# Two of the four float32 head tiles cast on chip before their TensorE transpose, and a planner that queues two engines on one PSUM bank

## Chip and metric

The kernel runs on one core of a Trainium2 chip. The metric is device time in microseconds (us); lower is better. Engines are named as in the profile: PE is TensorE (PEld its weight loads), DVE is VectorE, ACT is ScalarE, POOL is GpSimd, SP is the SyncE queue that issues most DMAs.

## What is computed

```python
batch, m, k, n = 16, 512, 1024, 768        # x, w1, w2: float32, drawn from randn
y1 = np.matmul(x, w1)
y2 = np.matmul(x, w2)
return (np.tanh(y1) * y2).astype(np.float32)
```

x flattened is 8192 x 1024; both products are 8192 x 768.

## The kernel before

**Tiles.** The 8192 rows are 64 row tiles of 128 (`mt`). A row tile must be transposed to `xT` (k on the partitions, 8 blocks of 128 columns) before TensorE can use it as the stationary operand. All products are in float16 and sum in float32 in eight PSUM banks of 128 x 512.

**Three stages.** Tiles 0 to 5 are the head and tile 63 the tail: their products are plain (`m{mt}{t}{F|G|M}{k}`: t is the weight matrix, F its first 512 columns, G its last 256, M both G parts side by side, k one of 8 slices). Tiles 6 to 62 go in 19 triples. A triple is 3 x 2 blocks of x (a row tile, half of k), the weights are 2 x 3 blocks of 512 columns (half of k; F of w1, F of w2, both G), and a scheme of 15 products of sums does the work of the plain 18: `A_SUMS` are sums of x blocks (`S{v}.{i}`, float16, DVE), `B_SUMS` sums of weight blocks (`B{v}`, once, DVE), and `C_OPS` is the list of what follows for each triple i: products `p*` (four matmuls each), `copy*` and `seed*` on ACT (a bank to SBUF, or a bank to another bank on which TensorE then accumulates), `add*` on DVE, and for each tile tanh (`t`, `th`, ACT) and multiplication (`m`, `mh`, DVE). In `C_OPS` names `c0` to `c10` are banks of a triple and `s...` SBUF tiles. Two entries matter here because they read the same bank: `t0` (ACT) and `add60` (DVE) both read `c0` after `p0`; in the same way `th1` (ACT) and `add4` (DVE) both read `c1` after `p3`. `p4` needs `add60`.

**The four ways of x onto the chip.** Tiles 0 to 3 are loaded as float32 (`Lx{mt}`, L332, by SP) and transposed by TensorE in float32 in two halves (`PT{mt}0`, `PT{mt}1`, L349: four transposes each into a bank of its own); each half is evacuated with a cast to float16 (`e{mt}0`, `e{mt}1`, L340 on ACT or L342 on DVE). Tiles 4 and 5 are loaded by POOL with a cast to float16 in the DMA (`L{mt}`, L382), transposed by TensorE in float16, eight transposes into one bank (`PT{mt}`, L359), and evacuated in one copy (`T{mt}`). Tiles 6 to 63 are loaded in the same way and transposed by DMA (L385, on SP). The POOL loads start behind a gate, which waits for weight slice b2 (L519). For each tile ACT sums the absolute values (`D{mt}`, L388), and for each weight slice too (`aw*`); these sums are needed only for a flag at the end, which chooses a general path for inputs out of range.

**Loads of the head.** In the order `x0 a0 x1 a1 x2 a2 x3 a3 a4 ... a7 b0 ... b7`, a0 to a3 from the ACT queue, the rest from SP, where a is w1 and b is w2 by k slices of 128 x 768 float32. Each slice is cast to float16 (`ca{k}`, `cb{k}`, L342 on DVE or L340 on ACT).

**The planner.** The order of the instructions on every engine is worked out in Python before the program is written, and pinned. `Planner.run` keeps a time for each engine; it offers every ready operation to each engine that may run it, with a duration for each engine, and takes the one that can start first. Between offers of equal start the engine listed first wins (`none, pe, act, dve, pool, sp`), and on one engine, among operations that start within 0.02, the one due first; ACT and DVE also hold back an operation for a more urgent one that becomes ready soon. The products of the triples keep one fixed order on TensorE (`PE_ORDER`); plain products of the tail tile may be put between the last of them (`FILL`) and are taken where the next fixed product can't start yet. A "chain" is the life of one PSUM bank: an operation that begins one takes the bank that was free first, and the bank comes free when the last operation of the chain has ended. Before the change the planner lets any two operations of one chain overlap that don't need each other. The durations it uses here:

```python
op(f"c{a}{k}", {"dve": 0.5, "act": 0.74}, ...)        # weight casts
op(f"e{mt}{h}", {"dve": 0.6, "act": 0.5}, ...)        # evacuation of half a float32 tile
op(f"T{mt}", {"dve": 0.67, "act": 0.93}, ...)         # evacuation of a float16 tile
```

What the planner does not write are the waits in the program: the tile framework adds those.

**Memory.** `xfpool` holds the float32 tiles in four rotating buffers; it is closed, with the pool of float32 weights, when the `pools` operation comes up in the plan, and the space is used for output tiles and `s...` tiles of the triples.

Of the kernel before, what the change touches and what calls it, by code (L numbers as in the profile page):

```python
# [77 lines left out]
class Planner:  # L78
# [13 lines left out]
    def op(self, name, engines, due, needs, fn, *args, behind=(), issued=(), chains=(), xfer=0.0, latency=None, seeds=False):  # L92


        assert name not in self.ops, name
        self.ops[name] = dict(engines=engines, due=due, needs=[n for n in needs if n], behind=[n for n in behind if n], issued=[n for n in issued if n], fn=fn, args=args,
                              chains=chains, xfer=xfer, latency=latency, seeds=seeds)
        for c in chains:
            self.chains.setdefault(c, {"left": 0, "bank": None, "end": 0.0})["left"] += 1

    def backward(self, margin):
        users = {n: [] for n in self.ops}
# [32 lines left out]
    def run(self, soon):  # L135
        free = {"none": 0.0, "pe": 0.0, "act": 0.0, "dve": 0.0, "pool": 0.0, "sp": 0.0}
        port = {"dve": 0.0, "pool": 0.0}
        bandwidth = 1.6
        left = {n: len(o["needs"] + o["behind"] + o["issued"]) for n, o in self.ops.items()}
        ready_at, end, engine_of, start_of = dict.fromkeys(self.ops, 0.0), {}, {}, {}  # L140
        ready = {e: [] for e in free}

        def release(n):
            for e in self.ops[n]["engines"]:
                ready[e].append(n)

        for n in self.ops:
            if not left[n]:
                release(n)
        position, lag = 0, 0.0  # L150
        strict = set(self.strict)
        while len(end) < len(self.ops):
            best = None
            for e, names in ready.items():
                options = []
                for n in names:
                    if n in strict and n != self.strict[position]:
                        continue
                    o = self.ops[n]
                    s = max(free[e], ready_at[n])  # L160
                    if n[0] in soon:
                        s = max(s, o["due"] + lag - soon[n[0]])
                    if e in port and n[0] in "SB":
                        s = max(s, port["dve" if e == "pool" else "pool"])
                    new = [c for c in o["chains"] if self.chains[c]["bank"] is None]
                    if new:
                        fit = self.fitting(o)
                        if not fit:
                            continue
                        s = max(s, min(fit)[0])  # L170
                    options.append((s, o["due"], n))
                if not options:
                    continue
                first = min(options)[0]
                s, due, n = min((o for o in options if o[0] <= first + 0.02), key=lambda o: o[1])
                ahead = max(0.4, self.LOOK * self.ops[n]["engines"][e])
                urgent = [o for o in options if o[0] < first + ahead and o[1] + lag < min(due + lag, o[0] + 1.0)]
                if urgent and e != "pe":
                    s, due, n = min(urgent, key=lambda o: o[1])
                if best is None or s < best[0]:  # L180
                    best = s, e, n
            if not best:
                held = [c for c, v in self.chains.items() if v["bank"] is not None and v["left"]]
                print("held", [(c, self.chains[c]["left"], [n for n, o in self.ops.items() if c in o["chains"] and n not in end][:4]) for c in held], free)
            assert best, ("stuck", [(n, self.ops[n]["needs"]) for n in self.strict[position:position + 3]])
            s, e, n = best
            o = self.ops[n]
            for c in o["chains"]:
                if self.chains[c]["bank"] is None:
                    entry = min(self.fitting(o))  # L190
                    self.bank_free.remove(entry)
                    self.chains[c]["bank"] = entry[1]
                    if not o["seeds"]:
                        (self.partial.add if c[0] == "T" else self.partial.discard)(entry[1])
            f = s + o["engines"][e]
            free[e] = f
            if e in port and n[0] in "SB":
                port[e] = f
            if o["xfer"]:
                bandwidth = max(bandwidth, f) + o["xfer"]  # L200
                done = bandwidth + (o["latency"] or self.LATENCY["cast" if e == "pool" else "sp"])
            else:
                done = f
            end[n], engine_of[n], start_of[n] = done, e, s
            for k in o["engines"]:
                ready[k].remove(n)
            if n in strict:
                position += 1
                lag = s - o["due"]
            for c in o["chains"]:  # L210
                chain = self.chains[c]
                chain["end"] = max(chain["end"], done + self.LATENCY[e])
                chain["left"] -= 1
                if not chain["left"]:
                    self.bank_free.append((chain["end"], chain["bank"]))
            for u in self.next.get(n, ()):
                ready_at[u] = max(ready_at[u], f)
                left[u] -= 1
                if not left[u]:
                    release(u)  # L220
            for u in self.users[n]:
                same = e in ("act", "dve", "pe") and e in self.ops[u]["engines"]
                slack = 1.0 if n in self.ops[u]["behind"] and self.ops[u]["xfer"] else 0.0
                ready_at[u] = max(ready_at[u], done + slack + (0.05 if same else 0.0 if o["xfer"] else self.LATENCY[e]))
                left[u] -= 1
                if not left[u]:
                    release(u)
        self.end, self.engine_of, self.start_of = end, engine_of, start_of
        return sorted(self.ops, key=lambda n: start_of[n])
# [3 lines left out]
def kernel(  # L233
# [18 lines left out]
    P = 128  # L252
    B, M, K = x.shape
    _, N = w1.shape
    KO = K // P
    KH = KO // 2
    MT = B * M // P
# [7 lines left out]
    WARM = 21  # L265
    SOON = {"S": 3.0, "D": 3.0}
    GATE = 2
    XH_FEW, XH_MORE = 3, ()
    POOL_FROM = 99
    BY_PE = 6  # L270
# [29 lines left out]

    head_stack = ExitStack()
    wfpool = head_stack.enter_context(tc.tile_pool(name="wf", bufs=WF_BUFS))
    xfpool = head_stack.enter_context(tc.tile_pool(name="xf", bufs=4))
    steady = {}

    pin = tc.keep_in_program_order
# [2 lines left out]
    op = plan.op  # L309
# [10 lines left out]
    def home(pool, key, shape, dtype):  # L320

        if (pool.name, key) not in fixed:
            fixed[pool.name, key] = pool.tile(shape, dtype, name=key)
        return fixed[pool.name, key]
# [3 lines left out]
        return xts[mt]  # L328

    def load_xf(e, mt):  # L330
        xfs[mt] = xfpool.tile([P, K], f32, tag="xf", name="x_f")
        pin(nc.sync.dma_start(xfs[mt], xf[mt]))  # L332

    def load_w(e, t, k, queue):
# [3 lines left out]
    def copy(e, dst, src):  # L338
        if e == "act":
            pin(nc.scalar.copy(dst, src))  # L340
        else:
            pin(engine[e].tensor_copy(dst, src))  # L342

    def cast_w(e, t, k):
        copy(e, wh[:, k, t * N:(t + 1) * N], wfs[t, k])

    def transpose_pe(e, mt, h, chain):
        for k in range(KH):
# [200 lines left out]
    for a, t, k in slices:  # L549
        op(f"c{a}{k}", {"dve": 0.5, "act": 0.74}, 6 + 1.3 * k + 9.5 * t,  # L550
           [f"L{a}{k}"], cast_w, t, k)
        op(f"aw{a}{k}", {"act": 0.92}, 80 + 10 * (t * KO + k), [f"c{a}{k}"], abs_w, t, k)
    for mt in range(4):
        for h in range(2):
            due = 5 + 2.3 * mt + 0.1 * h
            op(f"PT{mt}{h}", {"pe": 0.45}, due, [f"Lx{mt}"], transpose_pe, mt, h, ("T", mt, h), chains=[("T", mt, h)])
            op(f"e{mt}{h}", {"dve": 0.6, "act": 0.5}, due + 0.5, [f"PT{mt}{h}"] + ([f"e{mt}0"] if h else []), evacuate, mt, h,
               ("T", mt, h), chains=[("T", mt, h)])
        op(f"D{mt}", {"act": 1.05}, 30 + mt, [f"PT{mt}1"], abs_x, mt)

    PRODUCERS = {mt: [f"e{mt}0", f"e{mt}1"] if mt < 4 else [f"T{mt}"] for mt in range(MT)}
    xt_readers = {mt: [] for mt in range(MT)}

    def plain(mt, t, which, chain, due, at=0, first=True, behind=()):
        for k in range(KO):
            needs = ([f"cb{k}"] if t or which == "M" else []) + ([f"ca{k}"] if not t or which == "M" else [])
            needs.append(f"e{mt}{k // KH}" if mt < 4 else f"T{mt}")
            if not first and k == 0:
                needs.append(f"m{mt - 1}{t}{which}0")
            before = list(behind) + ([f"m{mt}{t}{which}0"] if k else [])  # L570
# [67 lines left out]
    for v, a, b, how in B_SUMS:  # L638
        needs = []
# [205 lines left out]
```

## Time and profile before

| what | value |
|---|---|
| time, median of 5 runs | 300.93 us (300.89 to 305.66) |
| time of the profiled execution | 303.9 us |
| span of its trace | 302.1 us |
| granted TensorE clock | 1.00 |
| PE busy | 293.2 us, 97% |
| DVE busy | 240.6 us, 80% |
| ACT busy | 220.2 us, 73% |
| POOL busy | 32.9 us, 11% |
| data moved | 64.80 MB, 214 GB/s mean |

The profile is of one execution. A row of its timeline has the start in us from the begin of the span, a duration, the engine, the line of the kernel, the operation, what it writes and reads by the program's names, shapes, and a count of merged instructions; in brackets, where the engine was idle before, how long and what ended that. Matmuls are pipelined: the duration of a row includes the last one's passage, so the stream's own pace is read from starts. A row of the windows view has a stretch of time, its length, the busy time and count of PE, PEld, DVE, ACT and POOL, the granted clock, the DMA share, and GB/s. In the page's slices each digit is the busy share of 1/40 of the span in tenths.

### The profile page before, as it was taken

To read this page: it belongs to the slowest core of one execution; us is meant where nothing else is said; L and a number is where in the kernel's file an instruction comes from. 1 tells how busy PE (TensorE), PEld (TensorE's weight loads), DVE (VectorE), ACT (ScalarE), POOL (GpSimd) and SP (SyncE) were. 2 spreads that over 40 slices of the span, in tenths; PEclk is the share of its full clock that TensorE was granted. 3 is DMA by queue.
4 is the path that set the end of the run, shared out by engine and by line. 5 is a ranking of instruction groups with operands and counts; after the bars stand their busy time and mean duration, and the time that the engine had idled before them with its cause. 6 is when DMAs were issued, how large, how long until landed. Compare 5 with 4: busy or idle time off the path is not lost. (4 is left out here: it accounts for less than half of the span.)

```text
span 302.1 us, 4458 instructions
## 1 busy us (share of the span) xinstructions
PE 293.2 (97%) x1418; PEld 138.9 (46%) x1418; DVE 240.6 (80%) x497; ACT 220.2 (73%) x438; POOL 32.9 (11%) x67
## 2 busy tenths in 40 slices
PE   8999999999999999799999999999999999999994
PEld 5656544444444444344444444444444444444442
DVE  1208999978988785988979779797898989888754
ACT  3879989998885965586777776778776777773641
POOL 0031220110101110201201101111010201000000
PEclk9999999999999999999999999999999999999999
DMA  7999999989999999999999999999999999995143
GB/s 291 407 400 189 167 162 183 178 164 206 193 209 161 232 259 82 127 298 221 273 233 207 197 199 177 293 213 191 234 205 227 204 207 225 211 378 204 69 176 125
DMA packets 82585, 64.80 MB, mean 214 GB/s; under 512 B 63616, under 2 KB 64128, under 8 KB 82560
## 3 DMA queue, kind: packets, MB, share of 16 engines
q1 hardware_dynamic: 73344, 47.20, 64.3%
q0 software_dynamic: 8640, 15.73, 35.6%
q10 hardware_dynamic: 576, 1.57, 1.3%
q8 instruction: 11, 0.18, 0.2%
q14 instruction: 14, 0.11, 0.2%
HBM read 39.85 MB, written 25.17 MB: 215 GB/s over the span
## 5 line engine op out<-in xcount | busy, mean ns | idle before, releaser
L475 PE MATMUL bank<-b,s 128*128 128x512 f16 x608 | 141.2, 379 | 2.4 <-DVE bank L490 2.3
L475 PEld LDWEIGHTS <-s 128*128 128x128 f16 x760 | 74.3, 98 | 92.8 <-issue 3.5
L490 DVE TENSOR_TENSOR bank<-bank,s 128x512 f32<-128x512 f32 x95 | 66.0, 695 | 26.4 <-ACT s L481 18.3
L481 ACT ACTIVATE s<-bank 128x512 f32<-128x512 f32 x95 | 55.2, 597 | 38.9 <-PE bank L475 38.9
L388 ACT ACTIVATE junk<-xh 128x1024 f16<-128x1024 f16 x60 | 63.4, 1056 | 3.0 <-DMA xh<-in_x_dram 2.8
L498 DVE TENSOR_TENSOR o<-o,bank 128x256 f32<-128x256 f32 (+1 forms) x114 | 61.1, 548 | 3.0 <-ACT o L493 2.4
L475 PEld LDWEIGHTS <-xT 128*128 128x128 f16 x380 | 37.1, 98 | 45.1 <-issue 0.8
L475 PE MATMUL bank<-b,xT 128*128 128x512 f16 x228 | 55.4, 379 | 0.0
L382 POOL DMA_DIRECT2D xh<-in_x_dram x60 | 32.1, 536 | 206.8 <-ACT o L493 63.1
L493 ACT ACTIVATE o<-bank 128x256 f32<-128x256 f32 x76 | 32.6, 437 | 11.9 <-DVE bank L490 8.6
L447 PE MATMUL bank<-wh,xT 128*128 128x512 f16 (+1 forms) x208 | 38.8, 338 | 1.4 <-ACT xT L340 0.7
L475 PE MATMUL bank<-wh,xT 128*128 128x512 f16 x152 | 39.0, 379 | 0.1
L475 PE MATMUL bank<-wh,s 128*128 128x512 f16 x152 | 39.0, 379 | 0.0
L432 DVE TENSOR_TENSOR s<-s,xT 128x512 f16<-128x512 f16 x76 | 31.7, 417 | 0.0
L447 PEld LDWEIGHTS <-xT 128*128 128x128 f16 x208 | 20.0, 98 | 18.3 <-ACT xT L340 1.4
L481 ACT ACTIVATE bank<-bank 128x512 f32<-128x512 f32 x38 | 21.0, 580 | 8.9 <-PE bank L475 7.1
L493 ACT ACTIVATE o<-s 128x512 f32<-128x512 f32 x38 | 23.8, 627 | 4.0 <-DVE s L490 3.2
L342 DVE CAST wh<-w_f 128x768 f16<-128x768 f32 x8 | 4.5, 565 | 18.6 <-DMA w_f<-in_w_dram 18.6
L432 DVE TENSOR_TENSOR s<-xT,xT 128x512 f16<-128x512 f16 x38 | 15.9, 418 | 0.1
L432 DVE TENSOR_TENSOR s<-xT,s 128x512 f16<-128x512 f16 x38 | 15.9, 418 | 0.0
L490 DVE TENSOR_TENSOR bank<-s,bank 128x512 f32<-128x512 f32 x19 | 13.1, 691 | 3.4 <-PE bank L475 2.9
L388 ACT ACTIVATE junk<-wh 128x768 f16<-128x768 f16 x16 | 13.5, 846 | 0.2
(39 smaller groups left out, 122.1 us busy)
## 6 DMA issues: line engine op xcount, KB each, us to landing
out_dram<-o SPq DMA_DIRECT2D x60, 384.0 KB, 5.4
xh<-in_x_dram POOLq DMA_DIRECT2D x60, 256.0 KB, 5.9
w_f<-in_w_dram SPq DMA_DIRECT2D x12, 384.0 KB, 8.2
x_f<-in_x_dram SPq DMA_DIRECT2D x4, 512.0 KB, 6.8
w_f<-in_w_dram ACTq DMA_DIRECT2D x4, 384.0 KB, 7.4
out_dram<-o SPq DMA_DIRECT2D x4, 256.0 KB, 2.2
xT<-xh SPq DMA_TRANSPOSE x58, 4.9
out_dram<-o SPq DMA_DIRECT2D x4, 128.0 KB, 1.8
```

What stands on the lines that cost most here:

```text
L342: pin(engine[e].tensor_copy(dst, src))
L382: pin(nc.gpsimd.dma_start(xhs[mt], xf[mt]))
L388: pin(nc.scalar.activation(junk[:, :src.shape[-1]], src, ACT.Abs, scale=scale, accum_out=sums[:, column:column + 1]))
L432: pin(engine[e].tensor_tensor(ss[i, v], x_operand(i, a), x_operand(i, b), OP[how]))
L447: pin(nc.tensor.matmul(b, xts[mt][:, k, :], rhs, start=first, stop=k == KO - 1, skip_group_check=True))
L475: pin(nc.tensor.matmul(place(i, dst), x_operand(i, a)[:, k, :], w_rhs(b, k), start=begins and k == 0, stop=k == KH - 1, skip_group_check=T ...
L481: pin(nc.scalar.activation(d, place(i, src), ACT.Copy, scale=float(sign)))
L490: pin(nc.vector.tensor_tensor(d, a, b, ALU.add if signs == (1, 1) else ALU.subtract))
L493: pin(nc.scalar.activation(out_tile(HEAD + 3 * i + r)[:, lo:lo + n], place(i, src)[:, :n], ACT.Tanh, scale=float(sign)))
L498: pin(nc.vector.tensor_tensor(o, o, place(i, src)[:, at:at + n], ALU.mult))
```

## The change

Tiles 2 and 3 (from `WIDE` = 2) are still loaded as float32, but then cast to float16 in SBUF (`X{mt}`, on DVE or ACT), transposed by TensorE in float16 as tiles 4 and 5 are (eight transposes into one bank), and evacuated in one copy (`T{mt}`). Their absolute sums read the float16 tile. The float32 tiles get fixed places instead of rotating buffers, and two float16 tiles lie beside them. In the planner, an operation that isn't TensorE's now starts no earlier than the end of the last operation that another engine (other than TensorE) did on the same chain.

```diff
--- before.py
+++ after.py
@@ -96,7 +96,7 @@
         self.ops[name] = dict(engines=engines, due=due, needs=[n for n in needs if n], behind=[n for n in behind if n], issued=[n for n in issued if n], fn=fn, args=args,
                               chains=chains, xfer=xfer, latency=latency, seeds=seeds)
         for c in chains:
-            self.chains.setdefault(c, {"left": 0, "bank": None, "end": 0.0})["left"] += 1
+            self.chains.setdefault(c, {"left": 0, "bank": None, "end": 0.0, "by": ""})["left"] += 1
 
     def backward(self, margin):
         users = {n: [] for n in self.ops}
@@ -162,6 +162,7 @@
                         s = max(s, o["due"] + lag - soon[n[0]])
                     if e in port and n[0] in "SB":
                         s = max(s, port["dve" if e == "pool" else "pool"])
+                    s = max([s] + [self.chains[c]["end"] for c in o["chains"] if self.chains[c]["by"] not in ("pe", "", e) and e != "pe"])
                     new = [c for c in o["chains"] if self.chains[c]["bank"] is None]
                     if new:
                         fit = self.fitting(o)
@@ -210,7 +211,7 @@
             for c in o["chains"]:
                 chain = self.chains[c]
                 chain["end"] = max(chain["end"], done + self.LATENCY[e])
-                chain["left"] -= 1
+                chain["left"], chain["by"] = chain["left"] - 1, e
                 if not chain["left"]:
                     self.bank_free.append((chain["end"], chain["bank"]))
             for u in self.next.get(n, ()):
@@ -265,6 +266,7 @@
     WARM = 21
     SOON = {"S": 3.0, "D": 3.0}
     GATE = 2
+    WIDE = 2
     XH_FEW, XH_MORE = 3, ()
     POOL_FROM = 99
     BY_PE = 6
@@ -300,7 +302,7 @@
 
     head_stack = ExitStack()
     wfpool = head_stack.enter_context(tc.tile_pool(name="wf", bufs=WF_BUFS))
-    xfpool = head_stack.enter_context(tc.tile_pool(name="xf", bufs=4))
+    xfpool = head_stack.enter_context(tc.tile_pool(name="xf", bufs=1))
     steady = {}
 
     pin = tc.keep_in_program_order
@@ -328,7 +330,7 @@
         return xts[mt]
 
     def load_xf(e, mt):
-        xfs[mt] = xfpool.tile([P, K], f32, tag="xf", name="x_f")
+        xfs[mt] = home(xfpool, f"xf{mt}", [P, K], f32)
         pin(nc.sync.dma_start(xfs[mt], xf[mt]))
 
     def load_w(e, t, k, queue):
@@ -343,6 +345,10 @@
 
     def cast_w(e, t, k):
         copy(e, wh[:, k, t * N:(t + 1) * N], wfs[t, k])
+
+    def cast_x(e, mt):
+        xhs[mt] = home(xfpool, f"xh{mt}", [P, K], f16)
+        copy(e, xhs[mt], xfs[mt])
 
     def transpose_pe(e, mt, h, chain):
         for k in range(KH):
@@ -550,7 +556,13 @@
         op(f"c{a}{k}", {"dve": 0.5, "act": 0.74}, 6 + 1.3 * k + 9.5 * t,
            [f"L{a}{k}"], cast_w, t, k)
         op(f"aw{a}{k}", {"act": 0.92}, 80 + 10 * (t * KO + k), [f"c{a}{k}"], abs_w, t, k)
-    for mt in range(4):
+    for mt in range(WIDE, 4):
+        due = 5 + 2.3 * mt
+        op(f"X{mt}", {"dve": 0.67, "act": 0.93}, due, [f"Lx{mt}"], cast_x, mt)
+        op(f"PT{mt}", {"pe": 0.5}, due, [f"X{mt}"], transpose_pe_h, mt, ("T", mt), chains=[("T", mt)])
+        op(f"T{mt}", {"dve": 0.67, "act": 0.93}, due + 0.5, [f"PT{mt}"], evacuate_h, mt, ("T", mt), chains=[("T", mt)])
+        op(f"D{mt}", {"act": 1.05}, 30 + mt, [f"X{mt}"], abs_x, mt)
+    for mt in range(WIDE):
         for h in range(2):
             due = 5 + 2.3 * mt + 0.1 * h
             op(f"PT{mt}{h}", {"pe": 0.45}, due, [f"Lx{mt}"], transpose_pe, mt, h, ("T", mt, h), chains=[("T", mt, h)])
@@ -558,13 +570,13 @@
                ("T", mt, h), chains=[("T", mt, h)])
         op(f"D{mt}", {"act": 1.05}, 30 + mt, [f"PT{mt}1"], abs_x, mt)
 
-    PRODUCERS = {mt: [f"e{mt}0", f"e{mt}1"] if mt < 4 else [f"T{mt}"] for mt in range(MT)}
+    PRODUCERS = {mt: [f"e{mt}0", f"e{mt}1"] if mt < WIDE else [f"T{mt}"] for mt in range(MT)}
     xt_readers = {mt: [] for mt in range(MT)}
 
     def plain(mt, t, which, chain, due, at=0, first=True, behind=()):
         for k in range(KO):
             needs = ([f"cb{k}"] if t or which == "M" else []) + ([f"ca{k}"] if not t or which == "M" else [])
-            needs.append(f"e{mt}{k // KH}" if mt < 4 else f"T{mt}")
+            needs.append(f"e{mt}{k // KH}" if mt < WIDE else f"T{mt}")
             if not first and k == 0:
                 needs.append(f"m{mt - 1}{t}{which}0")
             before = list(behind) + ([f"m{mt}{t}{which}0"] if k else [])
```

## The prediction

> **What bounds the kernel now.** I read the page's busy table and slices first, then the waits of PE, then the timeline around every pause of PE.
>
> ```profile
> PE 293.2 (97%) x1418; PEld 138.9 (46%) x1418; DVE 240.6 (80%) x497; ACT 220.2 (73%) x438; POOL 32.9 (11%) x67
> PE   8999999999999999799999999999999999999994
> PEclk9999999999999999999999999999999999999999
> ```
>
> TensorE is the bound, at full clock, so only its pauses and the columns it streams can be saved. Busy time hides short pauses, so I worked from starts: steady matmuls of 512 columns start 0.216 us apart, those of 256 columns 0.109, and what lies beyond that is a pause. After warm-up they are few: in the loads about 1.2 us in four pieces, 0.82 before 22.62, 0.16 at 54.6, some 2.8 between 120 and 132, 0.5 at 289.9.
>
> ```profile
> 113.00:121.00 8.00, 7.38 (x35) 3.23 (x33) 4.14 (x9) 4.70 (x10) 0.00 (x0) 1.00 1.30 91
> 122.31 2.89 PE L475 MATMUL bank<-b,s 128*128 128x512 f16 x12 [1.94 <-DVE bank L490]
> ```
>
> The 2.8 us follow eight microseconds in which the DMA moved 91 GB/s with a share of 1.30, against 246 GB/s in the eight before: a DMA transpose landed late, VectorE stood behind it, TensorE behind VectorE. This execution took 303.9 us (span 302.1); less 2.8 it is 301.1, next to the median of 300.93 of the timed runs. I take the pause as belonging to this execution alone, and make the sum from 300.93 with the other rows.
>
> ```profile
> 9.47 1.04 PE L349 MATMUL bank<-ident,x_f 128*128 128x128 f32 x8
> 9.94 0.56 DVE L342 CAST wh<-w_f 128x768 f16<-128x768 f32 x1 [1.70 <-DMA w_f<-in_w_dram]
> 10.10 1.07 ACT L340 CAST xT<-bank 128x512 f16<-128x512 f32 x2 [0.36 <-PE bank L349]
> ...
> 10.74 1.80 PE L447 MATMUL bank<-wh,xT 128*128 128x512 f16 x10 [0.24 <-ACT xT L340]
> ...
> 12.38 1.04 PE L349 MATMUL bank<-ident,x_f 128*128 128x128 f32 x8
> ...
> 20.27 1.81 ACT L340 CAST wh<-w_f 128x768 f16<-128x768 f32 x2 [1.67 <-DMA w_f<-in_w_dram]
> ...
> 21.98 3.16 ACT L453 ACTIVATE o<-bank 128x512 f32<-128x512 f32 x8
> ...
> 22.62 5.58 PE L447 MATMUL bank<-wh,xT 128*128 128x512 f16 x35 [0.65 <-ACT o L453]
> ...
> 28.04 0.61 PE L359 MATMUL bank<-ident_h,xh 128*128 128x128 f16 x8
> 28.49 4.06 PE L447 MATMUL bank<-wh,xT 128*128 128x512 f16 x24
> 28.69 0.69 DVE L342 COPY xT<-bank 128x1024 f16<-128x1024 f16 x1 [0.56 <-PE bank L359]
> ```
>
> Three things are to be seen. Until about 13 us TensorE waits for loads and for the steps behind a load. The restart at 22.62 is set not by TensorE: the first tanh, which frees a bank, stands on ScalarE behind two weight casts that wait for DMA. And from 22.62 on TensorE is dense.
>
> **Part 1, the transposes.** Eight float32 transposes hold TensorE for 0.87 us (12.38 to 13.25), eight float16 ones for 0.45 (28.04 to 28.49). Tiles 2 and 3 save 2 x 0.42 = 0.84 us of stream. The Trainium skill (TensorE: Matmul & The Clock Gate, Part 4) gives about 275 ns for one bf16 transpose in a kernel and says that transposes don't raise the clock; by that, 16 would cost an estimated 4.4 us, and the change would lose over 2. The rows show 8 in 0.45 at a granted clock of 9 tenths or more in every slice, and decide.
>
> What is added: per tile a cast of 128x1024 float32 to float16 and, for two evacuations of 512 columns (0.535 us each on ACT), one of 1024. No row has that cast. On DVE it lies between the 768-wide cast scaled (0.56 x 1024/768 = 0.75) and the 1024-wide copy (0.69): I take 0.7. On ACT the 1024-wide activations take 1.06 and the 768-wide casts 0.83: I take 1.06. Two things get later. The transposes wait for the cast, and the first products of a tile wait for the whole evacuation, where now the first half is enough.
>
> Walk through tile 2, whose data are there by 9.4. DVE is free: cast until 10.1, transposes with their last end at 10.7, copy on DVE until 11.4, first product at about 11.5 instead of 10.74. TensorE has only the four products of tiles 0 and 1 with the third weight slice in between. The planner gives that slice's cast to ACT (equal start, ACT is listed first; now ACT is busy with evacuation at that moment): 9.94 + 0.83 = 10.77, so four products from 10.85 (0.65 us), then six of tile 2 from 11.5 (0.98 us), done by 12.6 with a few hundredths between. Tile 3's load is due at about 11.5; both engines are free then, so the tie gives its cast to ACT, until 12.6; transposes until 13.1; the fourth weight cast stands behind it on ACT until 13.4, so TensorE goes on at 13.5, with the same 18 products done as before at 13.25. The eight products of tile 3, each reached behind others, don't wait again. So the 0.84 saved is eaten by 0.6 us before tile 2's transposes and 0.4 before the fourth slice, and TensorE is 0.2 later.
>
> What that is worth at 22.62: the pause of 0.82 before it absorbs the 0.2, since the tanh is not moved; but the planner then has about one product less (0.216 us) to put ahead of the wait, and that one comes afterwards. So 0 to +0.2; I take +0.1. From below: if a different order put the first tanh ahead of the casts, the pause and the saving would both come, -0.8. From above: if casts or evacuations queue on ACT, +0.5. DVE takes one cast and one copy in a stretch where it is busy 0.5 of 2 us; ACT ends up with about 1.6 us more, which pushes one absolute sum (0.86) later. Such sums are needed only by the final flag, so nothing waits for it. Loads, gate and DMA transposes stay where they are.
>
> **Part 2, the planner's rule.** It adds no instruction. Which pairs does it touch? The tanh `t0` (ACT) and the add `add60` (DVE) both read bank c0 once `p0` is done; `th1` and `add4` share c1. Elsewhere data already order the two engines.
>
> ```profile
> 53.05 1.49 DVE L490 TENSOR_TENSOR bank<-bank,s 128x512 f32<-128x512 f32 x2
> 53.20 0.61 ACT L493 ACTIVATE o<-bank 128x512 f32<-128x512 f32 x1
> ...
> 54.59 1.02 PE L475 MATMUL bank<-wh,xT 128*128 128x512 f16 x4
> ...
> 288.35 1.03 PE L475 MATMUL bank<-wh,s 128*128 128x512 f16 x4
> 288.55 0.60 ACT L493 ACTIVATE o<-bank 128x512 f32<-128x512 f32 x1 [0.48 <-PE bank L475]
> 289.18 0.70 DVE L490 TENSOR_TENSOR bank<-bank,s 128x512 f32<-128x512 f32 x1 [1.24 <-ACT o L493]
> 289.21 0.38 PE L447 MATMUL bank<-wh,xT 128*128 128x512 f16 x1
> 289.93 1.89 PE L475 MATMUL bank<-b,s 128*128 128x512 f16 x8 [0.34 <-DVE bank L490]
> ```
>
> The program already serialises them: the add starts 0.03 us after the tanh ends (289.18 after 289.15). The old planner doesn't know, and arranges everything else as if they ran together. The rule therefore changes only what is put into the wait.
>
> At the end this pays. `p4` of the last triple waits for that add; TensorE has one product of the last row tile ahead of it and then pauses 0.5. A planner that knows of the 0.6 us puts three more in (3 x 0.216 = 0.65), which are then missing from the 17 products after 295.5. VectorE's last steps follow one another closely, so I take -0.4, between -0.5 and 0.
>
> At 54.6 TensorE waited 0.16 for a bank that the add released. The planner will now fill VectorE's wait with a sum (next one 0.33 later), which puts the add at 53.98 instead of 53.84: +0.14; from -0.16 (pause gone) to rival 1.
>
> From 130 to 285 TensorE has no pause, whichever of the two came first; I take 0.
>
> **Sum:** 300.93 + 0.1 + 0.14 - 0.4 = 300.8.
>
> **Rivals.**
> 1, slower: the sum put ahead of `add60` holds its bank longer, and `p10` of the next triple takes just that bank. Price 0.14 to 0.33 us each time. It decides where no other bank is free 0.3 us earlier; the trace has this once in 18 triples. VectorE is busy 2.00 of 2 us from 34 to 38 and 9.60 of 10 from 50 to 60, so the first triples could all fall into it, and a late sum then delays the next: 5 x 0.33 = 1.6, time 302.4.
> 2, faster: a different order on ACT frees the first bank earlier; -0.8 with the tail's -0.4: 299.7.
> 3, the rule does nothing, since the order was already enforced: then the head's +0.1 alone, 301.0, within no change.
>
> **How the numbers follow.** Two tenths of a per cent, about what a measurement of this kernel can tell, are 0.6 us. My forecast with rival 3 lies within: 0.48. Rival 1 and other new pauses of a reordered plan: 0.28. Rival 2, with smaller gains: 0.24. The range goes to both rivals' prices, 299.8 to 302.4; for the likeliest case alone it is 300.4 to 301.4.
>
> **What would show it.** Right: sixteen float32 transposes instead of 32 and TensorE dense only from about 13.5; a first tanh near 22.0 still behind casts; the tail's pause filled by four products. Wrong: a first tanh near 21, or pauses before `p10` in several triples. A median that holds the DMA stall in most runs would also break the starting figure.

## The result, and the profile after

The changed kernel takes **302.15 us** (median of 50 runs, lowest 301.82) against 301.16 for the kernel before (94 runs on the same chips, lowest 300.69). The ratio of the means, without three runs that took over 1.5% longer than the fastest of their kernel, is 1.0025, 95% interval [1.0014, 1.0036]: slower by about a quarter of a per cent, where 300.8 and no measurable change were forecast. The profiled execution took 302.03 us, its span is 300.2.

The page of the changed kernel:

```profile
PE 292.3 (97%) x1418; PEld 138.8 (46%) x1418; DVE 239.8 (80%) x496; ACT 221.7 (74%) x439; POOL 32.7 (11%) x67
PE   8899999999999999999999999999999999999993
PEclk9999999999999999999999999999999999999999
```

By this page nothing went wrong: the same share of TensorE, full clock, no dip in the middle. The last slice is 3 where it was 4. The stretch that held the DMA stall before, in the windows view:

```profile
113.00:121.00 8.00, 8.00 (x38) 3.63 (x37) 6.87 (x15) 5.72 (x12) 1.58 (x3) 1.00 1.01 182
```

TensorE is busy 8.00 of 8 us where it was 7.38, and by starts it has no pause over 0.05 us behind the one that ends at 22.48, so this execution has no stall. The head, in the timeline (in this excerpt and the next two, rows of weight loads, PEld, are left out without a mark; `...` stands for other rows):

```profile
9.57 1.05 ACT L342 CAST xh<-xf 128x1024 f16<-128x1024 f32 x1
10.52 0.83 ACT L342 CAST wh<-w_f 128x768 f16<-128x768 f32 x1
10.67 0.62 PE L365 MATMUL bank<-ident_h,xh 128*128 128x128 f16 x8 [0.48 <-ACT xh L342]
11.33 1.01 ACT L342 COPY xT<-bank 128x1024 f16<-128x1024 f16 x1
...
11.83 0.69 DVE L344 CAST xh<-xf 128x1024 f16<-128x1024 f32 x1 [3.38 <-DMA xf<-in_x_dram]
...
12.40 1.15 PE L453 MATMUL bank<-wh,xT 128*128 128x512 f16 x6 [0.18 <-ACT xT L342]
13.38 0.61 PE L365 MATMUL bank<-ident_h,xh 128*128 128x128 f16 x8
13.83 8.29 PE L453 MATMUL bank<-wh,xT 128*128 128x512 f16 x49
...
22.48 6.01 PE L453 MATMUL bank<-wh,xT 128*128 128x512 f16 x37 [0.37 <-ACT o L459]
```

Cast and evacuation of tile 2 are both on ScalarE, the cast of tile 3 is on VectorE; the first product of tile 2 starts at 12.40 (10.74 before), TensorE is dense from 13.83 (13.25 before), and it restarts at 22.48 (22.62 before), again when a tanh on ScalarE frees a bank. The tail:

```profile
285.69 1.03 PE L481 MATMUL bank<-wh,s 128*128 128x512 f16 x4
285.89 0.60 ACT L499 ACTIVATE o<-bank 128x512 f32<-128x512 f32 x1 [0.48 <-PE bank L481]
286.52 0.70 DVE L496 TENSOR_TENSOR bank<-bank,s 128x512 f32<-128x512 f32 x1 [1.25 <-ACT o L499]
286.56 1.03 PE L453 MATMUL bank<-wh,xT 128*128 128x512 f16 x4
...
287.42 1.89 PE L481 MATMUL bank<-b,s 128*128 128x512 f16 x8
...
290.37 0.58 ACT L459 ACTIVATE o<-bank 128x512 f32<-128x512 f32 x1
290.85 0.59 ACT L487 ACTIVATE bank<-bank 128x512 f32<-128x512 f32 x1
...
291.75 1.89 PE L481 MATMUL bank<-b,xT 128*128 128x512 f16 x8
...
295.09 1.01 DVE L463 TENSOR_TENSOR o<-o,bank 128x512 f32<-128x512 f32 x2
```

The row of 285.69 is `p13` of the last triple, followed by the tanh `t0`, the add `add60`, four products of tile 63, `p4` at 287.42, tile 63's first tanh (290.37), the copy that prepares the bank of `p3` (`seed16`, 290.85), `p3`, and VectorE's last two evacuations. The kernel before has copy and tanh the other way round:

```profile
292.95 0.58 ACT L481 ACTIVATE bank<-bank 128x512 f32<-128x512 f32 x1
293.45 0.59 ACT L453 ACTIVATE o<-bank 128x512 f32<-128x512 f32 x1
...
293.82 1.89 PE L475 MATMUL bank<-b,xT 128*128 128x512 f16 x8
...
298.42 0.42 DVE L457 TENSOR_TENSOR o<-o,bank 128x256 f32<-128x256 f32 x1 [0.26 <-PEq L747]
```

The four products fill the old pause, as forecast. Yet the chain of waits now ends so (start, duration, engine, what, line):

```profile
289.31 2.60 PE bank L453 x16
291.91 0.88 PE bank L481 x4
292.79 0.02 issue
292.81 0.39 ACT o L499
293.20 0.02 issue
293.23 0.70 DVE bank L496
293.92 0.49 DVE o L504 x2
294.41 0.35 issue
294.76 0.41 DVE o L504
295.17 0.61 DVE o L463
295.78 0.02 DVEq L758
295.80 0.30 DVE o L463
```

From 292.79 on it leaves TensorE: the end hangs on `p3`, a tanh, a subtraction and VectorE's last multiplies and additions, one behind the other, and then on the stores. The time from a store's issue to its landing (shortest, median, longest of the last five), before and then after:

```profile
DMA to landing us min/median/max: 1.7/2.2/2.3
DMA to landing us min/median/max: 1.7/2.7/2.8
```

**A ledger of the span.** Every kernel here does the same work on TensorE after `p13` of the last triple: `p13` itself, `p4` and `p3` with one more product behind each, and 31 products of tile 63. So each profiled span can be cut at two points: the start of that `p13` (all of head and middle) and the end of VectorE's last evacuation. The experiments of the next section stand in it too.

| kernel | `p13` starts | to the last evacuation's end | to the span's end | median us |
|---|---|---|---|---|
| before | 288.35, 285.55 less the stall of 2.8 | 10.49 | 3.28 | 301.16 |
| after | 285.69 | 10.41 | 4.15 | 302.15 |
| e1 rule only | 285.70 | 10.41 | 4.13 | 301.66 |
| e2 float16 only | 286.50 | 10.49 | 3.10 | 301.61 |
| e3 rule not in last triple | 286.26 | 10.49 | 3.25 | 301.20 |
| e4 rule in last triple only | 287.02 (1.3 of stall) | 10.41 | 3.98 | 301.88 |
| e5 after, GATE 3 | 286.06 | 10.41 | 4.14 | 302.11 |
| e6 after, `t0` late | 285.91 | 9.92 | 3.55 | 300.98 |
| e7 before, `t0` late | 285.54 | 9.99 | 3.37 | 300.78 |
| e8 after, last store by ACT | 286.17 | 10.40 | 3.58 | 301.67 |
| e9 after, `seed16` first | 286.60 | 9.98 | 4.21 | 301.82 |
| e10 float32, rule, `t0` late | 287.09 (1.6 of stall) | 9.92 | 3.58 | 300.96 |
| e11 e10, two casts on DVE | 285.16 | 9.92 | 3.62 | 300.59 |
| e12 e11 with float16 tiles | 286.27 | 9.92 | 3.55 | 301.51 |
| e13 e12 once more | 285.93 | 9.93 | 3.55 | 301.40 |
| e14 e11, GATE 3 | 285.36 | 9.92 | 3.55 | 300.47 |
| e15 e11, last store by ACT | 285.05 | 9.93 | 3.19 | 300.09 |
| e16 e12, GATE 3 | 285.42 | 9.93 | 3.47 | 300.59 |
| e17 e15, GATE 3 | 287.35 (2.4 of pauses) | 9.92 | 3.23 | 299.93 |

From before to after: +0.14 up to `p13`, -0.08 to the last evacuation, +0.87 behind it. In this pair the loss lies where TensorE has nothing left to do. Each row is one execution, though, and the changed kernel's starts `p13` earliest of all rows with float16 tiles and the gate on b2: e2, e3, e6, e8 and e9, with the same head, have 285.91 to 286.60. The part on the head comes back to this.

### The profile page after: what moved, and what is told of

Same layout as the page of the kernel before. It is cut to its first block, busy times and chain, and to the rows that moved or that the text cites. A ratio compares the mean times of both kernels' runs of the same rounds, so it can differ in the third digit from the quotient of the medians.

```text
span 300.2 us, 4471 instructions
## 1 busy us (share of the span) xinstructions
PE 292.3 (97%) x1418; PEld 138.8 (46%) x1418; DVE 239.8 (80%) x496; ACT 221.7 (74%) x439; POOL 32.7 (11%) x67
## 4 chain that ended last, share of the span: by engine, by line
PE 90%; DMA 6%; DVE 1%; ACT 1%; ACTq 0%; issue 0%; SPq 0%; DVEq 0%
PE bank L481 82%; PE bank L453 8%; DMA w_f<-in_w_dram 6%; ACTq L338 0%; DVE o L463 0%; DVE o L504 0%; PE bank L365 0%; ACT wh L342 0%; DVE bank L496 0%; ACT o L459 0%; ACT o L499 0%; SPq L338 0%; PE bank L519 0%; DVEq L758 0%
## 5 line engine op out<-in xcount | busy, mean ns | idle before, releaser
L499 ACT ACTIVATE o<-bank 128x256 f32<-128x256 f32 x76 | 33.3, 438 | 11.8 <-DVE bank L496 7.5
L344 DVE CAST wh<-w_f 128x768 f16<-128x768 f32 x5 | 2.8, 560 | 14.2 <-DMA w_f<-in_w_dram 14.2
L394 ACT ACTIVATE junk<-wh 128x768 f16<-128x768 f16 x16 | 13.5, 846 | 0.2
```

Of the source, the lines that this page charges most:

```text
L394: pin(nc.scalar.activation(junk[:, :src.shape[-1]], src, ACT.Abs, scale=scale, accum_out=sums[:, column:column + 1]))
L499: pin(nc.scalar.activation(out_tile(HEAD + 3 * i + r)[:, lo:lo + n], place(i, src)[:, :n], ACT.Tanh, scale=float(sign)))
```

## Experiments

The kernels of one call ran beside runs of the kernel before on the same chip, whose medians were 301.1 (e1 to e4), 301.18 (e5 to e8), 301.25 (e9 to e12), 301.26 (e13 to e15) and 301.46 (e16, e17). My theory T was that the rule's order in the last triple costs the time; the rival H that the float16 tiles cost it at the head.

### One part at a time (e1 to e4)

e1 keeps the planner's rule and sets `WIDE = 4` (no float16 tiles). e2 keeps the float16 tiles and drops the rule. e3 and e4 split the rule, e3 with float16 tiles and e4 without:

```diff
-... for c in o["chains"] if self.chains[c]["by"] not in ("pe", "", e) and e != "pe"])
+... for c in o["chains"] if c[0] != 18 and self.chains[c]["by"] not in ("pe", "", e) and e != "pe"])   # e3
+... for c in o["chains"] if c[0] == 18 and self.chains[c]["by"] not in ("pe", "", e) and e != "pe"])   # e4
```

> The planner's rule with all four head tiles as before. Theory T (the 1.0 us is lost in the last triple: the products put ahead of p4, and the tanh of the tail tile put ahead of seed16, delay p3 and with it the five last stores by about 0.7 us): 0.7 to 0.9 us over the kernel before, about 301.9; the five stores start later against the 13th product's start than before. Theory H (the float16 path of tiles 2 and 3 costs it, through its extra cast): as the kernel before, 301.1, or 0.2 to 0.4 faster for the pauses filled. Theory M (the rule costs in the triples before the last): about 302, with pauses or a slower pace before 285 us.

> Tiles 2 and 3 on the float16 path, planner without the rule. Theory T: the head alone, +0.1 to +0.2 us, about 301.3. Theory H: about 302.1, all of the loss. Theory M: 301.1 to 301.3.

> The changed kernel with the rule left off for the banks of the last triple alone. Theory T: nearly all comes back, about 301.3. Theory H: 302.1, as the changed kernel. Theory M: 302.1, as the changed kernel.

> The kernel before with the rule for the banks of the last triple alone. Theory T: about 301.9, like the rule for all triples. Theory H: 301.1 or up to 0.4 less. Theory M: 301.1.

Ratios to before: e1 1.0012 [0.9998, 1.0026] (by the medians +0.56), e2 1.0004 [0.9978, 1.003], e3 0.9994 [0.9972, 1.0016], e4 1.0046 [1.001, 1.0082]. The changed kernel without the rule in its last triple (e3) is 0.95 us below it, and the kernel before with nothing but the rule in its last triple (e4) is 0.78 above its own before. Theory T holds for the last triple. In the earlier triples the rule is no loss: e2 to e3 is -0.41, e4 to e1 -0.22, both inside the intervals. The float16 tiles cost about 0.5 by the medians (before to e2, e1 to after), more than T's 0.15, with intervals that overlap. H as it stood, that the tiles cost all of it, is out by e3, which has them; but by the medians the two parts of the change cost about the same, 0.56 for the rule as a whole (e1) and 0.51 for the tiles (e2), where T had 0.7 to 0.9 and 0.15.

### Inside the last triple (e6 to e9)

If T is right, another order of the same operations must give the time back. In e6 the tanh `t0` of the last triple is put behind `add60`, so that `p4` waits for the add alone; e7 does the same to the kernel before:

```diff
-                   behind=reuse_out(mt), chains=chains)
+                   behind=reuse_out(mt) + ([f"add60.{i}"] if (name, i) == ("t0", TRIPLES - 1) else []), chains=chains)
```

> The changed kernel, in the last triple alone the tanh t0 ordered behind add60, which so runs at once. Theory T (the end hangs on the chain add60, p4, copy60, add52, seed16, p3 and the last stores): p4 no longer waits, seed16 ahead of the tail tile's tanh: 0.9 us back from leaving the rule off there and 0.4 to 0.6 more from the tanh, about 300.7. Rival P (the end is set by TensorE's stream): no more than 0.2 us from 302.1, since TensorE had no pause there.

> The kernel before with the same single order. Theory T: 0.5 to 0.6 us less, about 300.5: p4 starts 0.5 earlier and all stores of the last triple with it. Rival P: 0.4 less at most from the filled pause of 0.5, with the last stores where they were.

e6 is 300.98 (ratio 0.9986 [0.9963, 1.0009]), 1.17 below the changed kernel; e7 is 300.78 (0.999 [0.9968, 1.0012]), 0.40 below before. In e6 `p4` follows `p13` by 1.08 us (after: 1.73) and `p3` follows `p4` by 3.89 (after: 4.33). The two differences make 1.09, but the last evacuation comes only 0.49 earlier (9.92 against 10.41), since more products are left behind `p3`; another 0.60 is the shorter stretch behind the last evacuation (3.55 against 4.15). Its chain of waits ends:

```profile
288.88 2.17 PE bank L453 x13
291.05 1.73 PE bank L481 x8
292.77 2.62 PE bank L453 x17
295.39 0.02 issue
295.41 0.42 DVE o L463
```

TensorE is back to the last product, with one evacuation behind it; in the changed kernel the chain left it 3.3 us before the last evacuation ended.

e9 asks what of this is the order on ScalarE alone: tile 63's tanh is put behind `seed16`.

```diff
-               behind=reuse_out(mt), chains=[chain])
+               behind=reuse_out(mt) + ([f"seed16.{TRIPLES - 1}"] if mt == MT - 1 else []), chains=[chain])
```

> The changed kernel, with the tail tile's first tanh ordered behind seed16 of the last triple; t0 and add60 as in the changed kernel. The delay of p3 against p13 is 0.59 us there. Theory Q (0.43 of it is ACT's order, the rest the wait of p4): p3 0.4 us earlier, time 301.7. Rival F (the three products put ahead of p4 are the delay): no change, 302.1.

`p3` comes 3.89 behind `p4` again and the last evacuation 0.43 earlier (9.98), but the median falls only by 0.33, to 301.82 (1.0025 [1.0006, 1.0044]): the stretch behind the last evacuation is no shorter than in the changed kernel (4.21 against 4.15).

e8 goes at that stretch. The last store of tile 63 (its G part) is issued by ScalarE's queue, where SP's queue has four other stores just ahead.

```diff
-        pin(nc.sync.dma_start(of[mt][:, lo:lo + n], out_tile(mt)[:, lo:lo + n]))
+        pin((nc.scalar if mt == MT - 1 and lo == F else nc.sync).dma_start(of[mt][:, lo:lo + n], out_tile(mt)[:, lo:lo + n]))
```

> The changed kernel with the very last store issued by ScalarE instead of SP, so that it doesn't queue behind the one before it. Theory D (the end is the drain of five stores that start with the first): no change, within 0.2 us of 302.1. Rival S (SP's issue of the last store, 0.46 us behind the store before it, sets the end): 0.4 us less, 301.7.

301.67 (1.0004 [0.9983, 1.0025]), 0.48 below the changed kernel, and the stretch falls from 4.15 to 3.58. In the trace the last row of output data lands 2.51 us after the last evacuation in the changed kernel (296.10 to 298.61) and 1.88 in e8 (296.57 to 298.45); in before it was 1.64. So most of what was lost there is not the bulk of the five stores, since the same five are moved. The row of the store in e8, and the landing of its five:

```profile
296.61 0.36 ACTq L447 DMA_DIRECT2D out_dram<-o  x1
DMA to landing us min/median/max: 1.7/2.0/2.2
```

The traces show more than the theory asked. Each of these transfers lands in sixteen parts, with a record of each. In the changed kernel fifteen parts of the last store land within 2.02 us of its issue and the sixteenth 0.64 later; in before these are 1.73 and 0.20, in e8 2.15 and 0.06. So the +0.87 is made of a later issue (0.13), fifteen slower parts (0.29) and one late part (0.44), and what e8 takes back is the late part.

### The head (e5, e10 to e14, e16)

In the float16 kernels, all but e8, weight block b2 lands 1.0 to 1.3 us earlier than in before (20.24), so the gate of the loads of x, which waits for it (`GATE = 2`), opens earlier too; the loads of x then compete with the last weight blocks. Block 7 is cast at 26.65 (25.39 with the gate on b3), VectorE's sums behind it and the first addition of the G parts (`muF0`) are later, and TensorE waits for that bank near 33 us. e5 sets `GATE = 3` in the changed kernel.

> The changed kernel with the gate of POOL's x loads on weight slice b3 instead of b2. In the kernels with the float16 path the gate opened at 19.0 us instead of 20.4, and the last weight slice was there at 26.7 to 27.3 instead of 25.3. Theory G (the head's 0.5 us comes from the earlier gate: x loads in the way of b4 to b7, then VectorE's sums and the release of a bank late): cast of b7 back at about 25.5, first product of the triples 0.3 to 0.4 us earlier, time about 301.7. Rival C (the cast's own latency until 13 us costs it): no change, 302.1, since nothing before 13 us moves.

302.11 (1.002 [1.0003, 1.0036]): nothing, although the block's cast went back. TensorE's pause near 33 was only 0.045 us in the profiled changed kernel (0.35, 0.36 and 0.56 in e2, e3 and e9), and e5, which has none, still starts `p13` at 286.06.

e10 to e12 take the late `t0` and ask the question again. e10 has float32 tiles and the rule. e11 adds that the casts of blocks 2 and 3 of w2 go to VectorE, so that the tanh which frees the first bank doesn't stand behind them on ScalarE:

```diff
-        op(f"c{a}{k}", {"dve": 0.5, "act": 0.74}, ...
+        op(f"c{a}{k}", {"dve": 0.5} if t == 1 and k in (2, 3) else {"dve": 0.5, "act": 0.74}, ...
```

e12 is e11 with the float16 tiles (`WIDE = 2`).

> The rule with all four head tiles as before and t0 of the last triple behind add60. If the parts add up (rule in the earlier triples -0.2 to -0.4, order in the last -0.4, head as before): 300.4, below both kernels. If the rule's gain in the earlier triples is only that of the profiled executions: 300.8, like the order alone.

> As e10, with the casts of weight slices b2 and b3 on DVE instead of ACT, so that the first tanh isn't queued behind them. Theory R (the restart near 22.7 us is set by the tanh behind the two casts): restart 0.7 to 0.9 us earlier, at 21.9, and up to 0.8 us off the time if VectorE and the DMA let it through: 299.6 to 300.2. Rival L (the next limit is the data of b2 to b7 or VectorE's sums): restart earlier, but the first product of the triples where it was, and the time as e10.

> As e11, with tiles 2 and 3 on the float16 path. If the float16 path's saved stream (0.84 us) is hidden only by the restart, it shows now: as e11 or up to 0.3 less. If it is lost before 13 us to the cast and the later evacuation: 0.2 to 0.5 more than e11.

e10 300.96 (0.9999 [0.9971, 1.0027]), e11 300.59 (0.9987 [0.9965, 1.001]), e12 301.51 (0.9997 [0.9978, 1.0016]). In e11 the pause near 22 is gone. e12 has none there either, but:

```profile
32.89 0.38 PE L453 MATMUL bank<-wh,xT 128*128 128x512 f16 x1
33.96 0.38 PE L453 MATMUL bank<-wh,xT 128*128 128x512 f16 x1 [0.69 <-DVE o L463]
```

From start to start 1.07 us where a product takes 0.216: a pause of 0.86, ended by `muF0`. So e12 has in full the pause that was 0.045 us in the changed kernel's profile, and the gate was tried on it, with theories L (the late block 7 is the cost) and F (the float16 tiles as such are). e13 was to do this, e14 does it without the float16 tiles.

> The kernel of e12 (float16 tiles, rule, t0.18 late, casts of blocks 2 and 3 on VectorE) with GATE 3 in place of 2. Open since e12: why the float16 tiles cost 0.92 us over e11 when the restart of the products near 22 is no longer late. Theory L (the late weight block): the products' only pause after 13 us in e12, 0.86 us at 32.89 before m40M0, is the cost; it comes of block 7's cast at 26.48. With GATE 3 the cast goes back to about 25.4, the pause falls under 0.2 us, and the median to 300.6 to 300.9. Theory F (the float16 head itself: products filled in later, and row tiles 2 and 3 later): the pause goes, but the median stays within 0.3 us of e12's 301.51.

> The kernel of e11 (float32 tiles, rule, t0.18 late, casts of blocks 2 and 3 on VectorE) with GATE 3. It has no pause of the products after 13 us, so theory L expects no difference over 0.2 us from e11's 300.59; a gate that opens later could also bring the loads of x behind it late: then slower by 0.3 us or more.

e13's constant had stayed at 2: it is e12 once more, at 301.40 (0.9998 [0.998, 1.0017]), and says only how well such a median repeats. e14 is 300.47 (0.9988 [0.9961, 1.0015]), as e11. e16 is e12 with the gate moved:

```diff
-    GATE = 2
+    GATE = 3
```

> e13 left the gate's constant at 2 and so ran e12's kernel a second time (301.51 and 301.40). Here the gate of the loads of x does wait for weight block 3 (GATE 3). Theory L: the cast of block 7 falls back from 26.48 to about 25.4, VectorE's sums of the weights and the first addition muF0 come about 1 us earlier, the products' pause at 32.9 (0.86 in e12, 0.63 in e13) falls under 0.1 us, and the median to 300.6 to 300.9. Theory F: the pause goes, but the median stays within 0.3 us of 301.45.

300.59 (0.9976 [0.9966, 0.9986]), 0.86 below the mean of e12 and e13. Block 7 and the first additions in the timeline of VectorE, first e12, then e16:

```profile
26.48 0.56 DVE L344 CAST wh<-w_f 128x768 f16<-128x768 f32 x1 [1.58 <-DMA w_f<-in_w_dram]
...
33.23 1.28 DVE L463 TENSOR_TENSOR o<-o,bank 128x512 f32<-128x512 f32 x2
```

```profile
25.31 0.56 DVE L344 CAST wh<-w_f 128x768 f16<-128x768 f32 x1 [0.39 <-DMA w_f<-in_w_dram]
...
32.06 1.28 DVE L463 TENSOR_TENSOR o<-o,bank 128x512 f32<-128x512 f32 x2
```

The block comes 1.17 us earlier, `muF0` 1.17 earlier, the pause is gone, and so is the time. L holds for e12. And with the same gate the float16 tiles cost 0.12 us by the medians (e14 to e16, in calls whose runs of before differ by 0.20; against their own before e16 is the better by 0.08), 0.06 by the start of `p13`: nothing that these runs can tell.

### The best version (e15, e17)

e15 is e11 with e8's store; e17 is e15 with the gate on b3.

> The kernel of e11 with the last store of row tile 63 issued by ScalarE's queue. Theory S (the last store's issue behind the four others on SyncE's queue sets the end): a gain of 0.2 to 0.5 us as in e8, 300.1 to 300.4 us, because its issue falls from about 0.7 us behind the last evacuation to about 0.4. Rival (the end is set by the evacuations of the last triple's tiles on VectorE now that the chain is shorter): within 0.15 us of e11.

> e15 (float32 tiles, rule, t0.18 late, casts of blocks 2 and 3 on VectorE, last store issued by ScalarE's queue) with GATE 3. Theory L: nothing there waits for block 7 after 13 us, so within 0.2 us of e15's 300.09. Rival: x comes later behind the later gate and the first products that need it wait: slower by 0.3 us or more. If it is faster by more than 0.2 us, the gate costs something that the products' pauses don't show.

e15 is 300.09 (0.9963 [0.9941, 0.9984]), e17 **299.93 (0.9956 [0.9944, 0.9968])**. Both beat both kernels, e17 by 1.5 us against before in its call and by 2.2 us against the changed kernel's median; between the two nothing is to be told. The stretch behind the last evacuation falls from 3.62 to 3.19 in e15. It isn't the issue, which comes 0.03 us after the last evacuation in both; fifteen parts of the store land 1.77 us after it in e11 and 1.80 in e15, and the sixteenth 0.49 later in e11 and 0.04 in e15. Neither kernel has the float16 tiles.

## Why the prediction was wrong

**The step that failed is the tail**, put at -0.4 ("At the end this pays"). The mechanism came as written: four products instead of one ahead of `p4`, no pause. What I didn't follow was the rest of the order that the planner makes once it knows of the wait. In its own terms, from the profiles:

- `p4` starts 1.73 us behind `p13` instead of 1.58: the four products hold it 0.15 us longer than the add did. Forecast: no cost.
- `p3` starts 4.33 us behind `p4` instead of 3.89 (+0.44): on ScalarE tile 63's tanh, ready earlier since its products were done earlier, goes ahead of the copy that `p3` needs. e9 takes just that back. I had put the three products forward and nothing that depends on them.
- From `p3` to the last evacuation 4.35 us instead of 5.02: -0.67. Six products are missing there, not three (11 are left of 17), since three more were put into the later wait for `p3`; TensorE's last product starts 1.09 earlier against `p3`, but VectorE's chain, which now sets the pace, gives only 0.67 of it. So to this point the account is -0.08 where I wrote -0.4.
- Behind the last evacuation 4.15 us instead of 3.28: **+0.87**. Tile 63's additions now come directly behind those of the last triple, so its stores do too: in before the last of the five was issued 0.03 us after its evacuation and its data took 1.6, in the changed kernel 0.16 after and 2.3, 0.44 of the 0.87 in one late part of sixteen. e8 takes 0.57 of it back by issuing that store from ScalarE. I costed no store at all.

In sum +0.79 for a forecast -0.4. (The starting figure was a little low as well: 300.93, where 94 runs have 301.16.) The premise behind it, "TensorE is the bound ... so only its pauses and the columns it streams can be saved", is false behind `p13`: filling the last pause of TensorE bought 0.08 us up to the last evacuation and lost more behind it, since the end had two other things to wait for. (e7, which takes the pause away and leaves the rest in order, has its last evacuation 0.50 earlier.) The rows of before had it in them: 17 products behind `p3` paced VectorE's last additions, and with them the stores.

**The head: right kind, too small.** I took +0.1 within 0 to +0.2. The medians say 0.5 for the float16 tiles in two pairs (before to e2, e1 to the changed kernel), 0.02 in a third (e10 to e6), 0.9 in e12, and 0.12 once the gate is later (e16). The term that was mis-sized is "TensorE is 0.2 later", with the "about one product less" that came of it. Tile 2's cast and copy went to ScalarE and tile 3's cast to VectorE, not the other way round: the cast at 9.57 stands behind an evacuation on ScalarE, the copy behind a weight cast, so the first product of tile 2 came at 12.40 instead of 11.5 and the dense stretch at 13.83 instead of 13.5. That is what I had put at +0.5 "if casts or evacuations queue on ACT". The restart near 22.5 is still behind ScalarE's casts, as forecast. Counted in products of 512 columns, 53 start before it in all five profiles with float32 tiles and the casts of b2 and b3 as before (before, e1, e4, e7, e10), and 51 in all seven with float16 tiles (the changed kernel, e2, e3, e5, e6, e8, e9); the restart itself is at 22.61 to 22.82 and 22.48 to 23.00. So two products (0.43 us) come afterwards, not one.

"Loads, gate and DMA transposes stay where they are" failed too: the gate opened at 18.96 instead of 20.30, block 7 came late, and TensorE paused near 33. In the profiled pair head and middle together cost 0.14, against my 0.24 (0.1 and 0.14 at 54.6); but that execution restarts earlier than the six others and has almost nothing of the late pause. Less their stalls the five float32 rows start `p13` at 285.4 to 285.7, the seven float16 rows at 285.7 to 286.6. That the gate is the excess is shown for e12 alone. In e5 and e8 block 7 isn't late (cast at 25.39 and 25.58) and `p13` still starts at 286.06 and 286.17, so there the products missing before the restart are the most likely cost; no run tests that by itself in the changed kernel.

**The transposes** were sized rightly: tile 3's eight in float16 hold TensorE from 13.38 to 13.83, 0.45 us, at a granted clock of 9 tenths or more in every slice. By the figure of the Trainium skill (TensorE: Matmul & The Clock Gate, Part 4) the change would, by estimate, have lost over 2 us; it lost 1.0, and e3, with all sixteen of these transposes in it, lost nothing (0.9994 [0.9972, 1.0016]).

**The wait at 54.6** was put at +0.14, from -0.16. It went to the lower end:

```profile
53.89 1.03 PE L481 MATMUL bank<-b,s 128*128 128x512 f16 x4
53.96 0.70 DVE L496 TENSOR_TENSOR bank<-bank,s 128x512 f32<-128x512 f32 x1
...
54.75 1.03 PE L481 MATMUL bank<-wh,xT 128*128 128x512 f16 x4
```

The add starts at 53.96 (forecast 53.98), but the products run without a gap (four in 0.86 us from 53.89). e4 and e7, which have no rule there, still pause 0.16 at that place.

**The stall of 2.8 us** I set down to that execution alone. Mostly right: e7, which has before's order up to the last triple, shows none in its profile; e4, with that same order, shows 1.3 us at the same place (120 to 130), and e10 and e17 have 1.6 and 2.4 us at others. It comes in some executions and not in others.

**The rivals.** Rival 1, pauses before `p10`, didn't happen: TensorE has no pause over 0.05 us behind 22.48. It had the sign right for a reason that wasn't there. Rival 3, that the rule does nothing, is refuted by e3 and e4. Rival 2, a different order on ScalarE that frees the first bank earlier, is not in this change, but e11 makes it by hand and gets 0.37 of the 0.8 that I gave it, by medians whose intervals overlap. The slower case had 0.28 in all, and I had no rival in which the filled wait itself costs time.

## What to carry to other kernels

A pause of the bound engine is worth filling only as far as that engine also sets the end; in the last microseconds cut the span at the last product, the last evacuation and the end, and follow every operation that the filling makes ready earlier, on every queue, down to the last store. When a planner learns of a constraint that the program already obeyed, nothing is saved by the constraint itself; its worth is the worth of the new order, to be read triple by triple (here a loss of 0.8 to 0.95 us in one of 19). And a load that comes earlier moves whatever is gated on it. One profile of each kernel can mislead: here the pair put nearly all of the loss at the end, the medians only about half.

## What the hardware showed that I had not expected

- Stores just behind one another on one queue cost more than their rows show. The issue takes 0.33 us when the queue is idle and 0.37 to 0.82 when the store before it was issued 0.42 to 0.50 us earlier (0.40 for the last one in the changed kernel, 0.74 for the last but one in e1), and the last data land 2.3 us after the issue instead of 1.6. The Trainium skill (DMA: Bandwidth & Descriptors, "Anatomy of one DMA") puts about 2 us of fixed cost on a DMA that GpSimd issues, mostly until the last write is confirmed. These stores are issued by SyncE; their last landing is confirmed 1.93 us (before) to 2.66 us (after) after the issue, which agrees in size, and e11 and e15, with the issue at the same point, show that 0.4 of it can be one part of sixteen.
- One late part has a companion in the trace. In before, b2 was in by 18.73 on fifteen parts and at 20.24 on the last, and from b2 on every weight block has a part 1.5 to 1.7 us late. A packet of 16 KB on the DMA queue that the profile calls `instruction` starts at 17.38 there and takes 1.09 us. In the changed kernel it starts at 18.57, and b3 is the first with a late part. In all nineteen profiles such a packet starts between 17.38 and 19.00 and the first late block is b2 or b3; that alone moves a gate by 1.5 us. The queue's rows, before (17.3 to 18.5 us) and after (18.5 to 19.8):

```profile
q8 instruction: 1, 0.02, 5.7%
q8 instruction: 1, 0.02, 5.3%
```

- The same at the end: in the changed kernel a packet of 8 KB of that kind starts at 296.10, amid the five stores, and stores two to five have a part 0.64 to 0.72 us late. In e8, e15 and e17, where ScalarE issues the last store, no such packet starts before the data of SP's stores are down, and no part is over 0.08 us late. That these packets hold up the late parts fits all of this but isn't shown, since the trace doesn't say which DMA engine carried which; nor is it known why another queue for one store moves them.
- ScalarE takes 1.05 us to cast 128x1024 from float32 to float16, VectorE 0.69 (9.57 and 11.83 in the changed kernel).
